# Second mixer of a two-layer streaming encoder: each projection weight split once for two or three blocks, queries kept in memory, all keys and values on chip, float32 values in column tiles

## The chip, the cores and the metric

The kernel runs on one core of a Trainium2 chip. The metric is the device time of one execution in microseconds (us). A core has a matmul engine (PE; its weight loads are shown as PEld), a vector engine (DVE), a scalar engine (ACT), a general engine (POOL), and a queue that issues the DMAs (SP). Each engine takes its own instructions in order and waits on semaphores for the others. Matmuls write to PSUM, from where DVE or ACT carry the results to the on-chip memory SBUF.

## The reference

Layer 0 is a gated linear recurrence with a feed-forward part, layer 1 a grouped-query attention over a sliding window with a feed-forward part. Each part normalises before and after. The change is in layer 1's attention and in the projections that feed it:

```python
k, v = jnp.split(rms_norm(x, kv_norm) @ w_kv, 2, axis=-1)
k = rope(k.reshape(B, T, B_KV_HEADS, B_HEAD_DIM), pos)
...
q = rope((h @ w_b_q[j]).reshape(B, T, B_Q_HEADS, B_HEAD_DIM), pos)
...
s = jnp.einsum('bnqkgd,bnskd->bnkgqs', q.astype(F32), k.astype(F32)) * (B_HEAD_DIM ** -0.5)
s = jnp.where(valid[None, :, None, None, None, :], s, -jnp.inf)
m = jnp.maximum(jnp.max(s, axis=-1, keepdims=True), sink)
p = jnp.exp(s - m)
denom = jnp.sum(p, axis=-1, keepdims=True) + jnp.exp(sink - m)
return jnp.einsum('bnkgqs,bnskd->bnqkgd', p / denom, v.astype(F32))
```

There are 1024 prompt frames and 32 sample frames, a model width of 1024, 16 query heads and 4 key/value heads of 64, a window of 128 frames in chunks of 64, everything in float32.

## The kernel before

The 1056 frames are cut into three blocks of 384, 384 and 288 columns (`BL`). A dense product in near-float32 accuracy is made of three matmuls in the type fp32r: both operands are split into a high part and a remainder, and high times high, high times remainder and remainder times high are summed (`mm_fm`, line 132; `mm_tm`, line 144). A weight comes in units of 128 x 1024 (512 KB): `wunit` loads one, ACT makes the high part `wh`, DVE the remainder `wl`; where a norm weight is multiplied in, this is done in four pieces of 256 columns (lines 97 and 98), else at once (lines 101 and 102). There are two buffers for loads (`wst`) and four each for `wh` and `wl`. Two units (`wpair`) make the weight of one projection of 256 output columns.

The second mixer begins at line 827 while the first feed-forward part (`f0`) still finishes block 2. For each block, `kproj` makes the keys of all four heads, `vproj1` the values of three row tiles, and `qproj` the queries of one key head (four query heads). Keys and queries go through `rope` (rotation: four products on DVE, two sums on POOL) and then through DRAM to reach the layout that the scores need. Each projection of a block splits its weight anew: 18 pairs in all. Keys have two buffers (`kb`), values six (`vt`), and a value is split into high part and remainder (`split_v`).

Attention takes 12 steps per block (four key heads g, three row tiles jl). `att_s` makes the scores of four query heads in plain float32, the two heads of an even and odd pair in two PSUM tiles (`sc`), first all of one tile, then all of the other; adds the mask by small bf16 matmuls (`mk`); takes maxima (`rm`), exponentials (`P`, ACT), sums and normalises `P` head by head. `att_t` transposes `P` and splits it (`pth`, `ptl`); `att_v` multiplies by the split values: one matmul gives 128 rows of which high and remainder parts stand in different halves, which ACT and DVE move and add (lines 1028 to 1031) before the result is split again (`xh`, `xl`). The step before is transposed and multiplied after the scores of the present one.

`plan` puts other work between: in block 0 the projections of block 1, in block 1 those of block 2 and the output projection `op1` of block 0, in block 2 the last query projection, the normalisation of block 0 and the output projection of block 1. The order in which each engine gets the instructions is made by a scheduler from this program order; pools decide what has to wait for a buffer.

Of the kernel before, what the change touches and what calls it, by code (L numbers as in the profile page):

```python
# [8 lines left out]
F32 = mybir.dt.float32  # L9
# [15 lines left out]
NB = 3  # L25
# [33 lines left out]
def build(nc, tc, I, O):  # L59
# [767 lines left out]
    apc, ap = pool("ap")  # L827
    kbs, kds, vts, cosin = [None] * NB, [None] * NB, [None] * 9, [None] * NB
# [4 lines left out]

    def split_v(vf, rows, vt):
        vv = vf[:rows].rearrange("p (g d) -> p g d", g=4)
        nc.scalar.copy(vt[:rows, :, 0:64], vv)
        nc.vector.tensor_tensor(vt[:rows, :, 64:128], vv, vt[:rows, :, 0:64].bitcast(F32), sub)
        return vt

    def rope(b, units, res):  # L840
# [25 lines left out]
    def kproj(b):  # L866
# [3 lines left out]
        yield from rope(b, wpair(I["wk"], 0, scale="kv"), r)  # L870
# [4 lines left out]
        kb = kbs[b] = ap.tile([128, 4, 512], F32, tag="kb", name="kb", bufs=2)  # L875
# [9 lines left out]
    def vproj1(b):  # L885
# [3 lines left out]
        units = wpair(I["wv"], 0, scale="kv")  # L889
        for jl in range(3):  # L890
# [4 lines left out]
            vf = tmp()[:, :256]  # L895
            nc.scalar.activation(vf[:rows], ps[:rows, :256], AF.Copy, scale=rts[b][:rows, jl:jl + 1])
            j = 3 * b + jl
# [4 lines left out]
            vts[j] = split_v(vf, rows, ap.tile([128, 4, 128], F32R, tag="vt", name="vt", bufs=6))  # L902
            if jl < 2:
                yield

    take(0)
    gk, gv = kproj(0), vproj1(0)
    go(gk)
    go(f0)
    go(gk, 2)  # L910
    go(gv)
    go(f0)
    go(gv)
    ap2c, ap2 = pool("ap2")
    mbc, mb = pool("mb1", "right")
    mbs[:] = [mb, mb, None]
    os = [None] * NB
    nx = [None] * NB
    with tc.tile_pool(name="aps", bufs=1, space=PSUM, reuse_waits="tile") as aps:
# [9 lines left out]
        vcf = tmp()[:, :256]  # L929
        nc.sync.dma_start(vcf, I["cv"])  # L930
        vc = split_v(vcf, 128, ap2.tile([128, 4, 128], F32R, name="vc"))
# [3 lines left out]
        qts = {}  # L935

        def qproj(b, g):
            W = BL[b][1]
            r = []
            yield from rope(b, wpair(I["wq"], g, scale="mix_pre1"), r)  # L940
            a = r[0]
            qd = tc.dram_tile([2, 2, 2, 32, W], F32, name=f"qd{b}_{g}")
            for hf in range(2):
                nc.sync.dma_start(qd[:, :, hf].rearrange("pi pr r t -> (pi pr) r t"), a[:, hf, :W])
            qt = ap2.tile([128, 2, W], F32, tag="qt", name="qt", bufs=4)
            nc.sync.dma_start(qt, qd.rearrange("pi pr hf r t -> (pr hf r) pi t"))
            qts[b, g] = qt

        def att_s(b, g, jl):
# [14 lines left out]
            pss = []  # L964
            for pr in range(2):
                ps = aps.tile([128, 512], F32, tag="sc", name="sc", bufs=2)
                pvw = ps.rearrange("p (h k) -> p h k", h=2)
                rsl = slice(pr * 64, pr * 64 + 64)
                for pi in range(2):
                    lhs = qts[b, g][rsl, pi, qs]  # L970
                    off = lo
                    for (kt_, k0, n) in keys:
                        nc.tensor.matmul(pvw[:rows, pi, off:off + n], lhs, kt_[rsl, g, k0:k0 + n],  # L973
                                         start=pi == 0 and off == lo, stop=samp, skip_group_check=True)
                        off += n
                if not samp:
                    if lo == 0:
                        nc.tensor.matmul(pvw[:, :, 0:64], mk[rsl, 0:128], mk[rsl, 128:256], start=False,
                                         stop=True, skip_group_check=True)
                    nc.tensor.matmul(pvw[:, :, 192:256], mk[rsl, 0:128], mk[rsl, 256:384], start=False,  # L980
                                     stop=True, skip_group_check=True)
                nc.vector.tensor_reduce(rm[:rows, pr:4:2], pvw[:rows, :, lo:kend], AX.X, ALU.max)
                pss.append(pvw)
# [13 lines left out]
            for hh in range(4):  # L997
                nc.vector.tensor_scalar(P[:rows, hh, lo:kend], P[:rows, hh, lo:kend], rs[:rows, hh:hh + 1], None, mult)  # L998
            return dict(b=b, g=g, rows=rows, qs=qs, vals=vals, lo=lo, P=P)

        def att_t(c):
            rows, P = c["rows"], c["P"]
# [3 lines left out]
            for (vt, n) in c["vals"]:  # L1006
# [5 lines left out]
                pth = ap2.tile([128, 512], F32R, tag="pth", name="pth", bufs=2)  # L1012
                ptl = ap2.tile([128, 512], F32R, tag="ptl", name="ptl", bufs=2)
                nc.scalar.copy(pth[:n, :N], ptp[:n, :N])
                nc.vector.tensor_tensor(ptl[:n, :N], ptp[:n, :N], pth[:n, :N].bitcast(F32), sub)  # L1015
                c["pt"].append((pth, ptl))

        def att_v(c):
            rows, g, qs, vals = c["rows"], c["g"], c["qs"], c["vals"]
            N = 4 * rows  # L1020
            oh, ol = os[c["b"]]
            pav = aps.tile([128, 512], F32, tag="pt", name="pav", bufs=2)
            for i, ((vt, n), (pth, ptl)) in enumerate(zip(vals, c["pt"])):
                nc.tensor.matmul(pav[:, :N], vt[:n, g, :], pth[:n, :N], start=i == 0, stop=False)  # L1024
                nc.tensor.matmul(pav[:, :N], vt[:n, g, :], ptl[:n, :N], start=False, stop=i == len(vals) - 1)  # L1025
            pw = pav[:, :N].rearrange("p (pi pr q) -> p pi pr q", pi=2, pr=2)
            ot = tmp()[:, :256].rearrange("p (a q) -> p a q", a=2)
            nc.scalar.copy(ot[0:64, :, :rows], pw[64:128, :, 0, :])
            nc.scalar.copy(ot[64:128, :, :rows], pw[0:64, :, 1, :])
            nc.vector.tensor_tensor(ot[0:64, :, :rows], ot[0:64, :, :rows], pw[0:64, :, 0, :], add)  # L1030
            nc.vector.tensor_tensor(ot[64:128, :, :rows], ot[64:128, :, :rows], pw[64:128, :, 1, :], add)
            nc.scalar.copy(oh[:, 2 * g:2 * g + 2, qs], ot[:, :, :rows])
            nc.vector.tensor_tensor(ol[:, 2 * g:2 * g + 2, qs], ot[:, :, :rows],
                                    oh[:, 2 * g:2 * g + 2, qs].bitcast(F32), sub)
# [3 lines left out]

        go(gv, 4)
        gq = [qproj(0, g) for g in range(4)]  # L1040
        for g in range(4):
            go(gq[g])
            if g in (1, 2):
                go(f0)
            go(gq[g])
        K, Vp, Q = {}, {}, {}
        for b in (1, 2):
            take(b)
            K[b], Vp[b] = kproj(b), vproj1(b)
            Q[b] = [qproj(b, g) for g in range(4)]  # L1050
# [14 lines left out]
        for b in range(NB):  # L1065
            os[b] = newx(b)
            prev = None
            for u in range(13):
                c = att_s(b, u // 3, u % 3) if u < 12 else None
                for f, n in plan[b][u]:  # L1070
                    go(f, n)
# [117 lines left out]
```

## Time and profile before

| what | us |
|---|---|
| median of 3 runs | 2756.64 |
| lowest and highest | 2746.61, 2760.08 |
| the profiled execution | 2753.39 |
| its span, first to last instruction | 2751.5 |

The profile is of one execution. A row of instructions names the line, the engine, the operation, what is written from what, the shapes and the count. A row of a timeline begins with its start in us from the span's start, then how long it took. In a row by group the busy time and the mean of one stand behind the bar, then the idle time before it and what ended that.

### The profile page before, as it was taken

How to read it: one execution, taken by the hardware profiler on the slowest of the kernel's cores; microseconds unless marked ns; L12 is line 12 of the kernel's file. 1: busy time of each engine (PE TensorE's matmuls, PEld its weight loads, DVE VectorE, ACT ScalarE, POOL GpSimd, SP SyncE). 2: the span in 40 equal slices, each digit the busy share in tenths (PEclk: the TensorE clock that was granted, in tenths of full speed). 3: DMA queues.
4: the chain of work that ended last, by engine and by line, in shares of the span. 5: the costliest groups of instructions: out<-in, count | busy, mean ns of one | idle time of the engine just before them, and what ended most of it. 6: DMA issues, size and time to landing. Idle time of an engine off the chain costs nothing. (4 is left out here: it accounts for less than half of the span.)

```text
span 2751.5 us, 44746 instructions
## 1 busy us (share of the span) xinstructions
PE 2613.9 (95%) x17528; PEld 2516.8 (91%) x17528; DVE 1613.5 (59%) x3770; ACT 1054.7 (38%) x2371; POOL 422.1 (15%) x648
## 2 busy tenths in 40 slices
PE   7999998998999999999997799989899999999997
PEld 6999997998999999999997777878899999999997
DVE  8777778778523333333478687987633333333466
ACT  5555555555332121212244365666332121212133
POOL 5442435232100000000133101111200000000012
PEclk9999998999999999999999899999899999999998
DMA  5332333334311111111245623323421111111254
GB/s 165 91 95 95 109 101 112 120 109 130 111 47 47 46 47 46 47 47 54 88 152 154 187 81 120 107 93 99 128 63 47 46 47 47 47 46 47 70 161 143
DMA packets 95644, 247.00 MB, mean 90 GB/s; under 512 B 10264, under 2 KB 46008, under 8 KB 95432
## 3 DMA queue, kind: packets, MB, share of 16 engines
q1 hardware_dynamic: 95432, 244.14, 28.8%
q8 instruction: 138, 2.26, 0.3%
q14 instruction: 74, 0.61, 0.1%
HBM read 220.01 MB, written 24.28 MB: 89 GB/s over the span
## 5 line engine op out<-in xcount | busy, mean ns | idle before, releaser
L132 PE MATMUL mm<-xh,wh 128*128 128x384 f32 (+1 forms) x3120 | 1031.1, 331 | 15.1 <-ACT xh L205 11.7
L132 PE MATMUL mm<-xh,wl 128*128 128x384 f32 (+1 forms) x3120 | 1021.3, 328 | 22.2 <-DVE wl L98 17.1
L132 PE MATMUL mm<-xl,wh 128*128 128x384 f32 (+1 forms) x3120 | 1021.8, 328 | 2.8 <-DVE xl L206 2.5
L132 PEld LDWEIGHTS mm<-xh,wl 128*128 128x128 f32 x3120 | 596.5, 191 | 29.6 <-DVE wl L98 22.7
L132 PEld LDWEIGHTS mm<-xh,wh 128*128 128x128 f32 x3120 | 596.8, 191 | 23.4 <-ACT xh L205 12.6
L132 PEld LDWEIGHTS mm<-xl,wh 128*128 128x128 f32 x3120 | 596.1, 191 | 10.3 <-DVE xl L206 7.3
L102 DVE TENSOR_TENSOR wl<-wst,wh 128x1024 fp32r<-128x1024 f32 (+1 forms) x301 | 371.4, 1236 | 255.0 <-ACT wh L101 253.3
L101 ACT CAST wh<-wst 128x1024 fp32r<-128x1024 f32 (+1 forms) x301 | 314.5, 1047 | 469.9 <-PE mm L132 413.6
L174 POOL TENSOR_TENSOR acc<-acc,tmp 128x384 f32<-128x384 f32 (+1 forms) x168 | 195.0, 1162 | 1834.4 <-ACT tmp L173 1824.4
L132 PE MATMUL mm<-gh,wl 128*128 128x384 f32 (+1 forms) x1056 | 342.4, 325 | 12.1 <-DVE wl L102 12.1
L132 PE MATMUL mm<-gh,wh 128*128 128x384 f32 (+1 forms) x1056 | 343.3, 326 | 3.9 <-ACT gh L283 2.8
L132 PE MATMUL mm<-gl,wh 128*128 128x384 f32 (+1 forms) x1056 | 343.1, 325 | 0.0
L328 DVE TENSOR_TENSOR mix<-mix,mm 128x384 f32<-128x384 f32 (+1 forms) x240 | 124.4, 520 | 237.1 <-PE mm L132 237.1
L281 DVE TENSOR_TENSOR tmp<-mm,rb 128x384 f32<-128x384 f32 (+1 forms) x132 | 68.8, 522 | 254.4 <-PE mm L132 254.3
L132 PEld LDWEIGHTS mm<-gh,wl 128*128 128x128 f32 x1056 | 200.0, 190 | 13.1 <-DVE wl L102 13.1
L132 PEld LDWEIGHTS mm<-gh,wh 128*128 128x128 f32 x1056 | 199.8, 189 | 5.7 <-ACT gh L283 3.8
L283 ACT CAST gh<-tmp 128x384 fp32r<-128x384 f32 (+1 forms) x132 | 64.2, 486 | 360.3 <-DVE tmp L282 360.3
L132 PEld LDWEIGHTS mm<-gl,wh 128*128 128x128 f32 x1056 | 200.1, 189 | 0.3 <-DVE gl L284 0.2
L144 PE MATMUL mm<-wh,xh 128*128 128x256 f32 (+1 forms) x648 | 187.0, 289 | 2.5 <-ACT vt L492 2.4
L280 ACT ACTIVATE tmp<-tmp 128x384 f32<-128x384 f32 (+1 forms) x132 | 65.8, 498 | 316.4 <-DVE tmp L279 316.4
L144 PE MATMUL mm<-wh,xl 128*128 128x256 f32 (+1 forms) x648 | 184.1, 284 | 0.0
L144 PE MATMUL mm<-wl,xh 128*128 128x256 f32 (+1 forms) x648 | 182.3, 282 | 0.5 <-DVE wl L98 0.5
(205 smaller groups left out, 3147.3 us busy)
## 6 DMA issues: line engine op xcount, KB each, us to landing
wst<-in_wfi SPq DMA_DIRECT2D x120, 512.0 KB
wst<-in_wfo SPq DMA_DIRECT2D x60, 512.0 KB
wst<-in_wfq SPq DMA_DIRECT2D x47, 512.0 KB
wst<-in_wi SPq DMA_DIRECT2D x24, 512.0 KB
wst<-in_wg SPq DMA_DIRECT2D x24, 512.0 KB
wst<-in_wao SPq DMA_DIRECT2D x24, 512.0 KB
wst<-in_wq SPq DMA_DIRECT2D x24, 512.0 KB
wst<-in_wbo SPq DMA_DIRECT2D x24, 512.0 KB
```

Source lines behind the costliest of these rows:

```text
L101: nc.scalar.copy(wh[:, s], st[:, s])
L102: nc.vector.tensor_tensor(wl[:, s], st[:, s], wh[:, s].bitcast(F32), sub)
L132: last_mm[0] = nc.tensor.matmul(ps[:, :W], w, x, start=i == 0, stop=i == n - 1)
L144: last_mm[0] = nc.tensor.matmul(ps[:rows, :256], x, w, start=i == 0, stop=i == n - 1)
L174: nc.gpsimd.tensor_tensor(acc[:, :W], acc[:, :W], q[:, :W], add)
L280: nc.scalar.activation(ta[:, :W], ta[:, :W], AF.Silu)
L281: nc.vector.tensor_tensor(tb[:, :W], pb[:, :W], rb[:, :W], mult)
L283: nc.scalar.copy(gh[:, c0:c0 + W], tb[:, :W])
L328: nc.vector.tensor_tensor(dst, dst, ps[:, :W], add)
```

## The change

It does six things.

1. A weight pair is made outside the projections and handed to them: one key weight and one value weight serve blocks 0 and 1, another pair block 2; each of the four query weights serves all three blocks. That is 8 pairs for 18.
2. Both key and value projections of blocks 0 and 1, then those of block 2, and eight of twelve query projections are made ahead of the attention. The four left (blocks 1 and 2, heads 2 and 3) are spread over block 0's steps; block 1's steps carry the output projection of block 0, block 2's its normalisation and the output projection of block 1.
3. Rotated queries stay in DRAM tiles (`qds`) until `qload` brings them, four buffers.
4. All three key blocks have their own buffer, all nine value tiles too; values are kept in float32 without a split.
5. Scores alternate between the two PSUM tiles, so between the lower and upper 64 rows of the array. The product with the values is in float32, with 64 columns of weights: even heads write the lower, odd heads the upper 64 rows of PSUM. `P` transposed is copied (`pts`), by ACT for the first value tile and by DVE for the second, and the result is split straight from PSUM.
6. `P` is normalised by one product over four heads.

```diff
-    def kproj(b):
+    def kproj(b, units):
...
-        yield from rope(b, wpair(I["wk"], 0, scale="kv"), r)
+        yield from rope(b, units, r)
...
-        kb = kbs[b] = ap.tile([128, 4, 512], F32, tag="kb", name="kb", bufs=2)
+        kb = kbs[b] = late_pool[b].tile([128, 4, 128 + W], F32, name=f"kb{b}")
...
-            vts[j] = split_v(vf, rows, ap.tile([128, 4, 128], F32R, tag="vt", name="vt", bufs=6))
+            vf = vts[j] = ap.tile([128, 256], F32, tag="vt", name="vt", bufs=9)
...
-            cosin[b] = [ap.tile([128, 384], F32, tag=t, name=t, bufs=1) for t in ("cosr", "sinr")]
+            cosin[b] = [rp[0].tile([128, W], F32, name=f"{t}{b}") for t in ("cosr", "sinr")]
...
-        a = ap.tile([128, 2, 384], F32, tag="ra", name="ra", bufs=1)
+        a = rp[0].tile([128, 2, 384], F32, tag="ra", name="ra", bufs=2)
...
+            for pi in range(2):
+                off = lo
+                for (kt_, k0, n) in keys:
+                    for pr in range(2):
+                        rsl = slice(pr * 64, pr * 64 + 64)
+                        nc.tensor.matmul(pss[pr][:rows, pi, off:off + n], qts[b, g][rsl, pi, qs],
+                                         kt_[rsl, g, k0:k0 + n], start=pi == 0 and off == lo, stop=samp,
+                                         skip_group_check=True)
...
-            for hh in range(4):
-                nc.vector.tensor_scalar(P[:rows, hh, lo:kend], P[:rows, hh, lo:kend], rs[:rows, hh:hh + 1], None, mult)
+            nc.vector.tensor_tensor(P[:rows, :, lo:kend], P[:rows, :, lo:kend],
+                                    rs[:rows].unsqueeze(2).broadcast_to([rows, 4, kend - lo]), mult)
...
-                nc.scalar.copy(pth[:n, :N], ptp[:n, :N])
-                nc.vector.tensor_tensor(ptl[:n, :N], ptp[:n, :N], pth[:n, :N].bitcast(F32), sub)
+                if i == 0:
+                    nc.scalar.copy(pts[:n, :N], ptp[:n, :N])
+                else:
+                    nc.vector.tensor_copy(pts[:n, :N], ptp[:n, :N])
...
-                nc.tensor.matmul(pav[:, :N], vt[:n, g, :], pth[:n, :N], start=i == 0, stop=False)
-                nc.tensor.matmul(pav[:, :N], vt[:n, g, :], ptl[:n, :N], start=False, stop=i == len(vals) - 1)
+                for pr in range(2):
+                    nc.tensor.matmul(pav[pr * 64:pr * 64 + 64], vt[:n, g * 64:g * 64 + 64], ph[:, :, pr, :],
+                                     start=i == 0, stop=i == len(vals) - 1, skip_group_check=True)
...
+        for i, q in enumerate(late):
+            plan[0][3 * i] = plan[0][3 * i + 1] = [(q, 1)]
+        p, o = OP[0], OP[1]
+        for u in (1, 2, 3, 4, 6, 7, 8, 10, 11, 12):
+            plan[1][u] = [(p, 1)]
+        plan[2] = {u: [(p, 1)] for u in range(6)}
+        for u in range(4, 12):
+            plan[2].setdefault(u, []).append((o, 1))
```

Three places show how the order moves. First DVE, in the query projections ahead of the attention; before, `wl` (L98) is the remainder of a query weight, and L858 to L861 are the rope:

```order
L98 SCALAR_TENSOR_TENSOR wl<-wst,pv,wh 128x256 x3
L858 TENSOR_TENSOR ra<-mm,cosr 128x384
L859 TENSOR_TENSOR tmp<-mm,sinr 128x384
L98 SCALAR_TENSOR_TENSOR wl<-wst,pv,wh 128x256 x5
L860 TENSOR_TENSOR tmp<-mm,sinr 128x384
L861 TENSOR_TENSOR ra<-mm,cosr 128x384
L98 SCALAR_TENSOR_TENSOR wl<-wst,pv,wh 128x256 x7
```

The same place with the change, from the end of the splits of the second query weight (rope is L855 to L858 there):

```order
L98 SCALAR_TENSOR_TENSOR wl<-wst,pv,wh 128x256 x12
L855 TENSOR_TENSOR ra<-mm,cosr_16603 128x384
L856 TENSOR_TENSOR tmp<-mm,sinr_16604 128x384
L857 TENSOR_TENSOR tmp<-mm,sinr_16604 128x384
L858 TENSOR_TENSOR ra<-mm,cosr_16603 128x384
L855 TENSOR_TENSOR ra<-mm,cosr_16692 128x384
L856 TENSOR_TENSOR tmp<-mm,sinr_16693 128x384
L857 TENSOR_TENSOR tmp<-mm,sinr_16693 128x384
L858 TENSOR_TENSOR ra<-mm,cosr_16692 128x384
```

Before, every rope stands between the eight pieces of the next weight; now two blocks are roped behind each other and the pieces stand in a bundle ahead of them.

Second PE, inside an attention step: transposes (`ptp`), scores (`sc`), masks (`mk`) and values (`pav`), before, in block 0:

```order
L1009 MATMUL ptp<-ident,P 128x128 x8
L973 MATMUL sc<-kb,qt 128x256 x2
L978 LDWEIGHTS mk
L978 MATMUL sc<-mk 128x2x64
L980 LDWEIGHTS mk
L980 MATMUL sc<-mk 128x2x64
L973 MATMUL sc<-kb,qt 128x256
L1024 MATMUL pav<-pth,vt 128x512
L1025 MATMUL pav<-ptl,vt 128x512
```

And with the change, in block 1:

```order
L1023 MATMUL ptp<-ident,P 128x128 x8
L983 MATMUL sc<-kb_16240,qt 128x256 x2
L1041 MATMUL pav<-pts,vt 64x256 x4
L983 MATMUL sc<-kb_16240,qt 128x256 x2
L993 LDWEIGHTS mk
L993 MATMUL sc<-mk 128x2x64
```

Four value matmuls of 512 columns over the whole array have become four of 256 columns over half of it each, the scores of both tiles stand together, and the masks follow behind them.

Third SP, which issues the DMAs, at the end of the projections ahead of the attention, before (`qd` is the DRAM copy of a query, `qt` the tile that the scores read):

```order
L944 DMA qd_1_16573<-ra 4x32x384 x2
L90 DMA wst<-in_wq 128x1024
L946 DMA qt<-qd_1_16573 128x2x384
L90 DMA wst<-in_wk 128x1024 x2
L944 DMA qd_2_16667<-ra 4x32x384 x2
L90 DMA wst<-in_wv 128x1024
L946 DMA qt<-qd_2_16667 128x2x384
```

With the change, after the second key weight:

```order
L90 DMA wst<-in_wq 128x1024 x2
L911 DMA qd_1_17067<-ra 4x32x384 x2
L957 DMA qt<-qd_1_17067 128x2x384
L911 DMA qd_1_17131<-ra 4x32x384 x2
L90 DMA wst<-in_wbo 128x1024
```

Before, each query is followed by the loads of a further weight; now two blocks' queries are written per weight, and the first weight of the output projection already stands there.

More of the change, by code (lines that the diff above doesn't have):

```diff
@@ L1026, in att_v @@
[L1026 to L1032, printed above, removed]
@@ L1047, in build, with wq @@
[L1047 to L1050, printed above, removed]
+        def wq(g):
+            return wpair(I["wq"], g, scale="mix_pre1")
+        uq = wq(0)
+        run(qproj(0, 0, uq))
+        qload()
+        go(f0)
+        run(qproj(1, 0, uq))
+        go(f0)
+        take(2)
+        uk = wpair(I["wk"], 0, scale="kv")
+        run(kproj(2, uk))
+        run(qproj(2, 0, uq))
+        uv = wpair(I["wv"], 0, scale="kv")
@@ L1069, in build @@
                 c = att_s(b, u // 3, u % 3) if u < 12 else None
-                for f, n in plan[b][u]:
+                if u % 3 == 0 and u > 0 and order:
+                    qload()
+                for f, n in plan[b].get(u, ()):
                     go(f, n)
```

141 lines of the change are left out of this document (69 added, 72 removed).

## The prediction

> **What bounds the kernel now.** I read the page first, then busy time by stretch, then the waits of the second mixer, then its instructions.
>
> ```profile
> span 2751.5 us, 44746 instructions
> PE 2613.9 (95%) x17528; PEld 2516.8 (91%) x17528; DVE 1613.5 (59%) x3770; ACT 1054.7 (38%) x2371; POOL 422.1 (15%) x648
> ```
>
> A PE that is 95% busy seems to leave nothing to win, but records of pipelined matmuls overlap: they last longer than they lie apart. What counts is the distance between starts. The next rows give, for each stretch, length, busy time of PE, PEld, DVE, ACT and POOL, granted clock, DMA share and GB/s:
>
> ```profile
> 1483.00:1560.00 77.00, 66.25 (x359) 60.36 (x357) 57.87 (x138) 33.67 (x84) 20.55 (x22) 0.91 0.57 170
> 1560.00:1912.00 352.00, 318.54 (x1900) 271.82 (x1899) 285.59 (x748) 222.28 (x674) 47.95 (x48) 0.94 0.34 104
> 1483.00:1912.00 429.00, 384.79 (x2257) 332.18 (x2255) 343.46 (x886) 255.96 (x757) 68.49 (x70) 0.94 0.38 116
> 1912.00:2000.00 88.00, 79.15 (x440) 75.34 (x440) 59.65 (x126) 36.53 (x70) 23.23 (x22) 0.86 0.40 122
> ```
>
> The change touches 1483 to 1912: a front of projections for block 0 (to 1560), then 36 attention steps with the other projections and out-projections as filler. DVE is busy 286 of the 352 us of the steps. In both parts PE waits for DVE and ACT:
>
> ```profile
> PE pav L1024 <- DVE ptl L1015: 16.0, 18, 5.0
> PEld mm L132 <- DVE wl L98: 15.5, 14, 5.6
> PE mm L132 <- DVE wl L98: 10.7, 10, 5.3
> PE sc L973 <- ACT P L992: 9.2, 3, 7.9
> ```
>
> These are totals, times and the longest wait: the split of a weight (wl), the split of the probabilities (ptl) and the exponentials (P). The granted clock of 0.91 to 0.94 comes on top, since PE's gaps lower it. So the mixer is bound by PE and DVE together, each held up by the other.
>
> PE's own need is read from starts, count and distance:
>
> ```profile
> 1498.87 0.28 PE L144 MATMUL mm<-wh,xh 128*128 128x256 f32 x1
> ...
> 1501.46 0.28 PE L144 MATMUL mm<-wh,xl 128*128 128x256 f32 x1
> ...
> 1587.11 1.13 PE L973 MATMUL sc<-kb,qt 64*128 64x256 f32 x4
> 1588.07 0.22 PE L978 MATMUL sc<-mk 64*128 64x128 bf16 x1
> 1588.13 0.22 PE L980 MATMUL sc<-mk 64*128 64x128 bf16 x1
> 1588.27 0.38 PE L144 MATMUL mm<-wh,xh 128*128 128x256 f32 x1
> ...
> 1738.29 0.30 PE L132 MATMUL mm<-xl,wh 128*128 128x288 f32 x1
> ...
> 1741.20 0.29 PE L132 MATMUL mm<-xh,wl 128*128 128x288 f32 x1
> 1741.33 1.04 PE L1009 MATMUL ptp<-ident,P 128*128 128x128 f32 x8
> 1742.30 1.24 PE L973 MATMUL sc<-kb,qt 64*128 64x256 f32 x6
> ...
> 1809.08 0.34 PE L132 MATMUL mm<-xh,wh 128*128 128x384 f32 x1
> ...
> 1812.44 0.34 PE L132 MATMUL mm<-xl,wh 128*128 128x384 f32 x1
> ```
>
> From first to last there are 22, 22 and 19 steps: 0.118 us for a 256-column matmul, 0.132 for 288, 0.177 for 384. Four float32 score passes take 0.96 us (1587.11 to 1588.07), 0.24 each; each float32 score matmul is two passes. Eight transposes take 0.97. A mask follows a mask after 0.06, but a full-array matmul follows a mask after 0.14: a change of tiling costs about 0.09.
>
> **The change, part by part.** Dense matmuls neither vanish nor appear; they move.
>
> *Front.* It now holds three key, nine value and eight query pieces: 384 matmuls of 384 columns (68.0 us), 144 of 288 (19.0) and 216 of 256 (25.5), 112.5 us. The order shows a weight split before the projection that needs it, and one split serving two or three projections. One switch is late: the second value weight takes the slots that the last query projection has just freed, about 0.5 + 0.5 us for the first piece on ACT and DVE and 8 pieces at 0.5 against 0.35 of PE work, 2.5 us. The DVE burst of the feed-forward's last normalisation (at most 16.5 us by the rows of L234, L235 and L206 below, which are for the wider block) now lies beside 144 value matmuls, 17 us, whose eviction is ACT's; if that cover failed, the longest wait on wl above, 5.3 us, would return. With 3 us, an estimate, for normalisation matmuls and small waits the front is **118 us**.
>
> *Queues.* SP takes its transfers in order. The front asks for 16 weight loads of 0.5 MB and, by the shapes, some 7 MB of keys, queries and spilled blocks: 15 MB in 118 us, 130 GB/s, below the 170 that the old front reached, so I cost it at nothing; were it not hidden, rival 3 is what it would look like. The query loads of later blocks stand before out-projection weights on SP and wait for one of four query buffers, free once the third step of a head group has its scores; two weight buffers are filled ahead of them. The rotation tables are loaded and scaled five times instead of three, on POOL, which is busy 21 of 77 us in the front.
>
> *Splits, ropes and evictions.* DVE and ACT have in the steps (line, shapes, count, busy us, mean ns):
>
> ```profile
> L98 DVE SCALAR_TENSOR_TENSOR wl<-wst,pv,wh 128x256 fp32r<-128x256 f32 x92 | 42.0, 495 | 2.0 <-ACT wh L97 1.8
> L97 ACT ACTIVATE wh<-wst,pv 128x256 fp32r<-128x256 f32 x91 | 39.7, 508 | 20.4 <-DMA wst<-in_wv 13.0 <-PE mm L132 4.3 <-PE mm L144 1.9
> L1015 DVE TENSOR_TENSOR ptl<-ptp,pth 128x512 fp32r<-128x512 f32 x60 | 39.5, 678 | 0.7 <-ACT pth L1014 0.3
> L982 DVE TENSOR_REDUCE rm<-sc 128x2 f32<-128x512 f32 x56 | 37.5, 683 | 5.9 <-PE sc L980 5.5
> ...
> L102 DVE TENSOR_TENSOR wl<-wst,wh 128x1024 fp32r<-128x1024 f32 x20 | 24.1, 1215 | 2.0 <-ACT wh L101 2.0
> ...
> L1031 DVE TENSOR_TENSOR tmp<-tmp,pav 64x256 f32<-64x256 f32 x32 | 13.6, 425 | 0.5
> L1030 DVE TENSOR_TENSOR tmp<-tmp,pav 64x256 f32<-64x256 f32 x32 | 13.1, 410 | 9.5 <-ACT tmp L1029 9.3
> ...
> L206 DVE SCALAR_TENSOR_TENSOR xl<-mixb,pv,xh 128x384 fp32r<-128x384 f32 x8 | 6.5, 817 | 0.0
> ...
> L235 DVE TENSOR_TENSOR mixb<-mixb,xo 128x384 f32<-128x384 f32 x8 | 5.0, 638 | 1.2 <-DMA xo<-xsb 1.2
> ...
> L234 DVE SCALAR_TENSOR_TENSOR mixb<-mixb,pv,rb 128x384 f32<-128x384 f32 x8 | 4.6, 606 | 0.0
> ```
>
> Out of the steps go all scaled splits (42.0 us of DVE, 39.7 of ACT), half of L1015 (about 20: one plain copy remains, on DVE for the second value tile only), L1030 and L1031 (26.7) and seven of eleven ropes (four operations of about 0.5, 14). DVE falls from 286 to about 183 us. ACT loses its splits and the two moves between halves, and falls further below PE.
>
> *One P operation for four.* The four old ones and the nearest row for the new shape, L102's 1.215 us for 1024 columns:
>
> ```profile
> 1744.85 1.13 DVE L998 TENSOR_SCALAR P<-P,rs 128x256 f32<-128x256 f32 x4
> ```
>
> The sum takes no change (bounds: 0.3 us less a step, four fixed costs saved, to 0.1 more). The Trainium skill speaks against this edit: VectorE: DVE Perf Modes, section "Mode 2×_2P — use both read ports for one tensor", says that a float32 operation with a scalar can run at two elements per cycle from SBUF and one with two tensors only at one, which by its 0.96 GHz is an estimate of 0.53 us before and 1.07 after, 17 us more DVE over the steps; by it the forecast would be some 2 us later, since DVE bounds only block 2's first steps. The trace disagrees for the old form: 0.28 us for 256 columns is one element per cycle.
>
> *Tiles on PE.* Scores now alternate between the two row halves, value matmuls between two column halves. No value matmul of this shape is in the trace; the nearest is the first mixer's float32 one with 64 columns of weights, alternating halves:
>
> ```profile
> 312.45 0.77 PE L672 MATMUL psB<-ZZ,K 128*64 128x96 f32 x12
> 313.00 0.42 PE L675 MATMUL psB<-Q,K 128*64 128x64 f32 x2
> ```
>
> Twelve passes of 96 columns start in 0.55 us, 0.046 each, where 0.24 x 96/256 = 0.090 would be serial: the halves run in pairs. I take pairs: eight passes fill five slots (one half starts a slot later), 1.2 us for values (four passes of 0.23 before, no gain) and 1.3 with masks for scores (2.1 before). Serial would be 1.9 and 2.1. A full step needs 1.3 + 0.97 + 1.2 = 3.5 us of PE; 28 full and 8 short steps (1.7) 112 us. The program order counts 185 changes of tiling against 123: 62 x 0.09 = 6 us more. Filler is 96 matmuls of 384, 96 of 288 and 384 of 384 (two out-projections): 98 us. Sum 216 us, so PE is the longest by 33.
>
> *What is left uncovered.* Steps without filler (seven in blocks 0 and 1) run at the loop score, maximum, exponentials, next score: 1.3 + 2 x 0.68 + four exponentials of about 0.46 + small work and hand-overs 0.8 = 5.3 against 3.5, 12 us. In block 2's first four steps block 0's normalisation (8 x (0.82 + 0.64 + 0.61) = 16.5 us of DVE) has no matmuls beside it: 16. Start and end: 6. Attention is **250 us**.
>
> *Sum.* The last feed-forward matmul starts at 1486.4, so before has 425.5 us to 1912; after 118 + 250 = 368. Out-projection tail (88 us) and all else keep their order: cost 0. The gain is 57: 2751.5 - 57 = 2694.5, with 2 us around the span (profiled execution 2753.4) **2696 us**. The median shown, 2756.6, lies 3 us higher. The transfers now taken once (20 loads of 512 KB fewer) gain nothing more by themselves.
>
> **The rivals.**
> 1. *PE near its floor*: uncovered parts shrink to 10, front 115: 341, 2669 us. For: DVE has 33 us to spare. Against: block 2 starts without matmuls.
> 2. *Tiles serial*: 1.5 us more a full step, 42: 2738. Against: L672.
> 3. *Front as ragged as before*: 1486.5 to 1560, 73.5 us, for one key, three value and four query pieces, 240 x 0.177 + 72 x 0.118 = 51 us, 1.44 times; 112.5 x 1.44 = 162, 44 more: 2740. For: it keeps the order split, project, rope on one DVE. Against: 8 splits for 20 pieces. Half of it: 2718.
> 4. *Slower: latency, not work, sets the step.* Before, 352 / 36 = 9.8 us a step with filler inside. If the chain of scores, maximum, exponentials, transposes and values keeps that, the projections moved forward are simply added: 118 + 352 = 470, 2798. It decides from (425.5 - 118) / 36 = 8.5 us a step. For: both score banks are now needed at once. Against: the chain above is 5.3, and the waits on ptl and wl lose their cause.
> That the change doesn't do what it says is excluded by the order: 64 scaled pieces per engine for 144, and paired tiles.
>
> **How the numbers follow.** Forecast 0.64 (2675 to 2722); rival 1 0.12; rival 2 0.07; rival 3 0.12, half of it at the half price; rival 4 0.05. Range 2658 to 2732: rival 1 and half of rival 3 inside, serial tiles and rival 4 outside. 0.5% is about what a measurement of this kernel tells from no change: 14 us. Faster 0.64 + 0.12 + 0.07 + half of rival 3 = 0.89; same 0.06; slower 0.05.
>
> **What would show it.** Right: a front of about 118 us with PE starts 0.177 apart and hardly a wait on wl; steps of 6.9 us on average; DVE about 183 us in the steps; eight value passes in about 1.2 us. Wrong: waits on wl between projections (rival 3), passes 0.24 apart (rival 2), scores waiting for P in steps with filler (rival 4).

## The result, and the profile after

The changed kernel takes 2711.0 us (median of 4 runs, 2708.0 to 2716.4) against 2755.4 us for the kernel before, now of 4 runs too. The ratio is 0.985, with a 95% interval of 0.983 to 0.987. The two medians lie 44 us apart, but by the ratio and by the traces below it is faster by about 40 us, where 57 were forecast. The page of the changed kernel begins so:

```profile
span 2714.5 us, 44432 instructions
PE 2602.9 (96%) x17664; PEld 2494.4 (92%) x17664; DVE 1534.2 (57%) x3464; ACT 977.3 (36%) x2177; POOL 428.1 (16%) x652
```

DVE lost 79 us and ACT 77, twice what the kernel gained: most of that work had been hidden. The next rows are busy time by stretch (length, busy us of PE, PEld, DVE, ACT and POOL, granted clock, DMA share, GB/s). The first is the front, from the start of the last feed-forward matmul to the first score, the second the 36 attention steps, the third the out-projection tail:

```profile
1493.65:1613.50 119.85, 116.46 (x767) 113.35 (x765) 72.94 (x162) 36.83 (x92) 37.42 (x40) 1.00 0.58 171
...
1613.50:1878.00 264.50, 247.00 (x1597) 186.79 (x1597) 186.54 (x407) 140.39 (x467) 37.07 (x32) 0.95 0.24 73
1878.00:1966.00 88.00, 79.42 (x447) 75.77 (x445) 60.14 (x126) 36.91 (x71) 23.26 (x22) 0.86 0.38 118
```

The front has grown as forecast and runs at the full clock; the steps have shrunk from 350 to 264 us. PE's waits in the front, and then PE's and its weight loads' in the steps (total, times, longest):

```profile
PE mm L189 <- DVE dm L185: 1.5, 2, 1.0
PE mm L132 <- DVE tmp L856: 1.2, 1, 1.2
PE mm L132 <- DVE wl L98: 0.7, 2, 0.3
```

```profile
PE ptp L1023 <- DVE P L1010: 5.4, 7, 2.2
PE pav L1041 <- DVE pts L1030: 4.3, 3, 2.2
PE pav L1041 <- ACT pts L1028: 2.4, 6, 0.8
```

```profile
PEld pav L1041 <- ACT pts L1028: 11.2, 28, 1.2
PEld sc L983 <- issue: 9.4, 32, 0.8
```

Almost nothing is left of the waits on the weight splits (10.7 us) and on the split probabilities (16.0). What is left are waits for the normalised P and for the copies of the transposes.

To compare traces I cut each at three instructions: the start of the last feed-forward matmul, of the first score and of the last value matmul.

| kernel | last FFN matmul | front | steps | front + steps | to the last matmul | median, us |
|---|---|---|---|---|---|---|
| before | 1486.4 | 73.6 | 350.4 | 424.0 | 830.3 | 2755.4 |
| after | 1493.6 | 119.8 | 264.1 | 383.9 | 826.1 | 2711.0 |
| E1 attention edits only | 1488.5 | 69.3 | 343.5 | 412.8 | 825.6 | 2741.9 |
| E2 unpaired order | 1486.5 | 119.6 | 277.6 | 397.2 | 825.8 | 2723.0 |
| E3 four P operations | 1487.0 | 120.1 | 262.5 | 382.6 | 827.1 | 2707.6 |
| E4 grouped order | 1483.2 | 119.7 | 286.0 | 405.7 | 827.8 | 2729.7 |
| E5 out-projection early | 1490.5 | 120.3 | 257.2 | 377.5 | 824.9 | 2702.0 |
| E6 one score tile | 1484.2 | 120.0 | 256.8 | 376.8 | 826.3 | 2701.9 |
| E7 = E5 and E6 | 1484.6 | 119.8 | 249.1 | 368.9 | 831.0 | 2695.7 |
| E8 matmuls of zeros added in the second feed-forward | 1481.9 | 119.9 | 266.5 | 386.4 | 872.4 | 2753.2 |
| E9 split for each projection | 1484.9 | 143.7 | 275.9 | 419.6 | 825.1 | 2745.1 |
| E10 = E7, copies on ACT | 1485.9 | 120.0 | 249.7 | 369.7 | 829.8 | 2697.3 |
| E11 ten loads more | 1490.0 | 130.8 | 268.8 | 399.6 | 825.0 | 2724.4 |
| E12 ten splits more | 1495.8 | 126.8 | 264.2 | 391.0 | 825.5 | 2720.2 |

Up to the first column every kernel issues the same instructions in the same order; its 14 us of scatter (1481.9 to 1495.8) are between executions. So the 7.2 us by which the profiled execution of after starts its front late are no effect of the change, nor are the 4.2 it gains at the end (824.9 to 831.0 over all but E8, whose added work lies there). The change itself is the fifth column: 424.0 - 383.9 = 40.1 us. Differences between kernels are read there below, and whole times beside them. E8 gives a measure for their scatter: up to the second feed-forward PE has the same instructions there as in the changed kernel, and they take 386.4 us against 383.9. Two or three us between two rows of this column therefore say nothing.

### The profile page after: what moved, and what is told of

Its sections match the earlier page's. It is cut to its first block, busy times and chain, and to the rows that moved or that the text cites. A ratio compares the mean times of both kernels' runs of the same rounds, so it can differ in the third digit from the quotient of the medians.

```text
span 2714.5 us, 44432 instructions
## 1 busy us (share of the span) xinstructions
PE 2602.9 (96%) x17664; PEld 2494.4 (92%) x17664; DVE 1534.2 (57%) x3464; ACT 977.3 (36%) x2177; POOL 428.1 (16%) x652
## 4 chain that ended last, share of the span: by engine, by line
PE 74%; DVE 15%; ACT 5%; DMA 4%; issue 2%; POOL 1%; SPq 0%; POOLq 0%; ACTq 0%; DVEq 0%
PE mm L132 63%; PE mm L144 5%; DVE wl L102 2%; ACT wh L101 1%; DVE xl L206 1%; PE sc L983 1%; PE pav L1041 1%; DVE wl L98 1%; DVE mixb L235 1%; DVE mix L234 1%; DVE mixb L234 1%; DVE mix L235 1%; PE ptp L1023 1%; PE po L729 1%; ACT P L1005 1%
## 5 line engine op out<-in xcount | busy, mean ns | idle before, releaser
L132 PE MATMUL mm<-gl,wh 128*128 128x384 f32 (+1 forms) x1056 | 343.5, 325 | 0.0
```

The costliest lines, as they stand in the source:

```text
L132: last_mm[0] = nc.tensor.matmul(ps[:, :W], w, x, start=i == 0, stop=i == n - 1)
```

## The experiments

The theory from the two traces: both halves of the change earn; the missing 14 us of the steps (264 where 250 were forecast) are changes of tiling on PE that cost more than the forecast's 0.09 us. The rival: PE's work is as forecast, and the latency of the chain from scores to values sets the pace.

**E1, one half alone.** The kernel before, with the attention edits only:

```diff
-            vf = tmp()[:, :256]
+            vf = vts[j] = ap.tile([128, 256], F32, tag="vt", name="vt", bufs=6)
...
-            vts[j] = split_v(vf, rows, ap.tile([128, 4, 128], F32R, tag="vt", name="vt", bufs=6))
```

`att_s`, `att_t` and `att_v` are those of the changed kernel.

> The kernel before with the attention half of the change alone: float32 values in column tiles, scores alternating between row halves, one P operation, no split of the probabilities; projections stay per block inside the steps. Theory A (both halves earn: the attention edits take about 46 us off DVE and pair the tiles, the projection edits take the scaled splits out of the steps): about 2735 us, half of the gain of 44. Rival B (only the projections matter): within 5 us of the kernel before, 2750 to 2760. Rival C (only the attention edits matter): 2705 to 2715, as the changed kernel.

Measured: 2741.9 us, ratio 0.996 (0.9945 to 0.998); front and steps lose 11.2 of the 40.1 us. Between A and B: the attention edits are worth something over a quarter, although they take 48 us off DVE in the steps, which now read as follows, with PE's waits behind:

```profile
1557.80:1901.30 343.50, 315.22 (x2024) 253.20 (x2024) 237.73 (x525) 181.55 (x564) 51.35 (x48) 0.93 0.34 106
```

```profile
PE sc L964 <- ACT P L986: 13.7, 4, 6.9
PE pav L1022 <- ACT pts L1009: 5.1, 8, 1.6
PE pav L1022 <- DVE pts L1011: 4.9, 4, 2.2
```

The waits of values have fallen from 16.0 to 10.0 and those of scores risen from 9.2 to 13.7. The seven longest waits of PE in the steps add up to 32 us before and to 27 here, so little of the 48 us that DVE no longer does was what PE waited for.

**E2, pairs undone.** In the changed kernel, scores and values again half after half:

```diff
-            for pi in range(2):
+            for pr in range(2):
+              for pi in range(2):
...
-                    for pr in range(2):
```

> The changed kernel with scores issued one row half after the other and values one column half after the other, as the scores were before. If the pairs run at the same time and PE sets the pace of the steps, 8 passes of 0.215 us take the place of 4 slots in scores and in values: 1.7 us a full step, 28 x 1.7 + 8 x 0.85 = 55 us at most, 30 to 55 us slower. If the chain scores, maximum, exponentials, transposes, values sets the pace (rival), the extra passes lie in PE's waits: under 15 us slower. If tiles did not pair at all: no change.

Measured: 2723.0 us, 13.3 us more in front and steps. That would speak for latency, but the trace shows that the edit was only half an undoing, since the instructions of the two halves were still ordered together where both were ready. Counting score and value passes that start within 25 ns of the one ahead: 88 and 136 pairs (of 160 and 136) in the changed kernel, 29 and 66 here. So 129 passes more have a slot of their own, at 0.209 us 27 us of PE, and 13 of them show. That is neither theory's extreme: about half of PE's additional work shows as time.

The count also shows that in the changed kernel itself 72 of the 160 score pairs do not form (E6, whose expectation takes 93 as formed where this count has 88).

**E3, the P operation undone.**

```diff
-            nc.vector.tensor_tensor(P[:rows, :, lo:kend], P[:rows, :, lo:kend],
-                                    rs[:rows].unsqueeze(2).broadcast_to([rows, 4, kend - lo]), mult)
+            for hh in range(4):
+                nc.vector.tensor_scalar(P[:rows, hh, lo:kend], P[:rows, hh, lo:kend], rs[:rows, hh:hh + 1], None, mult)
```

> The changed kernel with P normalised by four operations with a per-partition scalar, as before. By the row of before (four took 1.13 us) against the one operation of after (1.19 us mean): DVE busy in the steps within 3 us, time within 5 us of the changed kernel. If a float32 operation with a scalar ran at two elements per cycle: 17 us less DVE in the steps, 0.6 us an operation shorter, and about 2 us less time.

Measured: 2707.6 us; its interval (0.982 to 0.985) overlaps that of the changed kernel. The groups of P's normalisation, first of the changed kernel, then of this one (count, busy us, mean ns):

```profile
L1010 DVE TENSOR_TENSOR P<-P,rs 128x1024 f32<-128x1024 f32 x28 | 36.1, 1289 | 0.4
```

```profile
L1011 DVE TENSOR_SCALAR P<-P,rs 128x256 f32<-128x256 f32 x112 | 39.8, 418 | 0.5
```

28 steps take 1.29 us each in one operation and 39.8 / 28 = 1.42 in four, on average; where nothing disturbs them it is 1.22 (the median) and 1.14. The edit is worth nothing either way. The Trainium skill (VectorE: DVE Perf Modes, section "Mode 2×_2P — use both read ports for one tensor") would have the four at two elements per cycle, by an estimate 0.53 us a step; the measured 1.42, and 1.14 undisturbed, contradict it for this form.

**E4, fewer changes of tiling.** PE's order in the steps is fixed to whole groups, each queued behind the last matmul of the one ahead:

```diff
+                with after_dense():
                     c = att_s(b, u // 3, u % 3) if u < 12 else None
...
+                with after_dense():
                     for f, n in plan[b].get(u, ()):
                         go(f, n)
...
+                    with after_dense():
                         att_t(prev)
+                    with after_dense():
                         att_v(prev)
```

> The changed kernel with PE's order in the steps fixed to whole groups: scores and masks, projection or out-projection work, transposes, values. Changes of tiling fall from 184 to 110; no work is added or left out. Theory A (each change of tiling costs PE about 0.26 us, worked out as 266 us of the steps less 196 of matmuls at their distances less 21 of long waits, over 185 changes): 74 x 0.26 = 19 us less, of which the lost freedom to fill waits takes some back: 5 to 19 us faster than the changed kernel. Rival B (a change costs the 0.09 us of the prediction, and the chain's latency sets the pace): 7 us less PE work, more waits of values for the copies of the transposes: 0 to 25 us slower.

Measured: 2729.7 us, 22 us more in front and steps. PE's waits in the steps are now these:

```profile
PE pav L1041 <- ACT pts L1028: 15.0, 27, 1.4
PE ptp L1023 <- DVE P L1010: 10.9, 6, 3.5
PE sc L983 <- ACT P L1005: 9.7, 7, 4.5
PE pav L1041 <- DVE pts L1030: 8.4, 11, 2.0
```

The sum over PE's distances above 0.45 us between two starts, each less 0.26, rises from 21 us to 53; without it the steps fall from 243 to 233. Put down to the 74 changes less alone, these 10 us would be 0.13 each, half the 0.26 of theory A. But 128 score pairs form here where 88 did, which at 0.209 us a pass is 8 of the 10 us, so E4 leaves no clear price for a change; E8 gives one. Theory A falls as to size. What the grouping costs, 32 us more in long waits, is three times what it saves: PE needs the freedom to put projection work into a step's waits.

**E8, the price of a change measured by itself.** In the second feed-forward, where PE is the bound, matmuls of zeros are added into the running sums, in three shapes, one kind to a group of 24 (`m` counts groups):

```diff
+                    if probe[0] is not None and n == 24 and i in (8, 16):
+                        z, m = probe[0], probe[1] % 4
+                        if m == 1:
+                            nc.tensor.matmul(ps[:, 0:64], z[:, 0:128], z[:, 0:64], start=False, stop=False)
+                        elif m == 2:
+                            nc.tensor.matmul(ps[:, 0:64], z[0:64, 0:128], z[0:64, 0:64], start=False, stop=False)
+                        elif m == 3:
+                            nc.tensor.matmul(ps[0:64, 0:64], z[:, 0:64], z[:, 0:64], start=False, stop=False)
```

> The changed kernel with 66 additional bf16 matmuls of 64 columns of zeros of each of three shapes inside the first projections of the second feed-forward, where PE is the bound and the starts lie 0.177 us apart: on the whole array, on 64 rows, on 64 columns. The result doesn't change. A whole-array one should cost its own time, about 0.06 us. For one on half the rows or columns, two changes of tiling come on top: 0.24 us in all if a change costs 0.09 us (the prediction), 0.32 to 0.44 us if it costs 0.13 to 0.19 (the first matmul behind a change also starts its successor late, as the rows of the changed kernel look). The time rises by 36 us or by 46 to 62.

Measured: one run of 2753.2 us, 42 more. PE's timeline (start, duration) around one on half the rows, then around one on the whole array:

```profile
2014.67 0.33 PE L132 MATMUL mm<-xl,wh 128*128 128x384 f32 x1
2014.94 0.20 PE L139 MATMUL mm<-zt 64*128 64x64 bf16 x1
2015.07 0.44 PE L132 MATMUL mm<-xh,wl 128*128 128x384 f32 x1
2015.35 0.33 PE L132 MATMUL mm<-xh,wh 128*128 128x384 f32 x1
...
2046.40 0.33 PE L132 MATMUL mm<-xh,wh 128*128 128x384 f32 x1
2046.57 0.20 PE L137 MATMUL mm<-zt 128*128 128x64 bf16 x1
2046.61 0.42 PE L132 MATMUL mm<-xl,wh 128*128 128x384 f32 x1
2046.88 0.34 PE L132 MATMUL mm<-xh,wl 128*128 128x384 f32 x1
```

From the first row to the fourth it is 0.68 us with a change there and back, 0.48 without, 0.35 undisturbed. These are also the medians of the 44 of each kind that stand among matmuls of 384 columns; for half of the columns it is 0.70. A change costs (0.68 - 0.48) / 2 = 0.10 us, and 0.11 for columns: the forecast's 0.09 was right. The total of 0.24 that the expectation draws from it was not, at 0.33 and 0.35, because the small matmul alone costs 0.13 and not 0.06. This 0.13 has nothing to do with tiling: 0.04 is the matmul itself, and 0.09 comes because the matmul behind it holds PE for 0.27 until the next start instead of 0.175. The next weight load, 0.19 us long, would not fit beside a matmul of 0.04; that reading was not tested.

**E5, work beside block 0's normalisation.** Cut into pieces of 8 us, the start of block 2 stands out (columns as above):

```profile
1778.00:1786.00 8.00, 5.20 (x30) 3.12 (x29) 7.62 (x17) 5.19 (x16) 0.99 (x1) 1.00 0.30 97
1786.00:1794.00 8.00, 4.64 (x32) 2.59 (x30) 7.18 (x15) 4.70 (x15) 2.47 (x3) 0.59 0.29 100
1794.00:1802.00 8.00, 6.63 (x36) 4.07 (x36) 7.64 (x16) 4.51 (x16) 2.56 (x2) 0.77 0.31 101
1802.00:1810.00 8.00, 4.62 (x22) 3.15 (x22) 7.21 (x17) 3.95 (x14) 3.00 (x2) 0.65 0.32 98
1810.00:1818.00 8.00, 7.79 (x36) 7.59 (x36) 4.59 (x20) 2.53 (x11) 0.27 (x2) 0.71 0.00 0
```

In the first four rows DVE is busy over 7 of 8 us and PE 4.6 to 6.6; from 1786 the granted clock lies below 0.8, and it stays there until 1818, after DVE's pressure has ended. E5 puts block 1's out-projection there; its result takes the place of the key tiles of blocks 0 and 1, as the one buffer of that size is still in use:

```diff
-        for u in range(4, 12):
+        for u in range(0, 8):
             plan[2].setdefault(u, []).append((o, 1))
+        mixes[1] = lambda: Halves(*[ap.tile([128, 4, 512], F32, tag=f"kb{i}", name=f"mix1{i}") for i in range(2)])
```

> The changed kernel with block 1's out-projection matmuls in the steps u = 0 to 7 of block 2 instead of u = 4 to 11 (its result goes into the space of the key tiles of blocks 0 and 1, so that it need not wait for block 0's buffer). Same work. Theory A (in the first 45 us of block 2 DVE is the bound, since block 0's last normalisation, 16.5 us of DVE, has no matmuls beside it; PE waits there and its granted clock falls to 0.5 to 0.8): these steps cost no more with the matmuls inside, the later ones lose them, 5 to 12 us faster than the changed kernel, and the clock of block 2 near 1.00. Rival B (DVE's turn-around inside each step sets the pace, and matmuls in it only delay transposes and values): within 3 us, or slower by up to 10.

Measured: 2702.0 us, ratio 0.982 (0.980 to 0.983); the steps lose 6.9 us. The same stretch now reads:

```profile
1778.00:1786.00 8.00, 8.00 (x51) 6.45 (x51) 7.75 (x16) 5.32 (x17) 1.52 (x2) 1.00 0.32 101
1786.00:1794.00 8.00, 6.26 (x46) 4.83 (x44) 8.00 (x17) 7.11 (x19) 3.17 (x3) 1.00 0.42 141
1794.00:1802.00 8.00, 7.10 (x48) 6.28 (x48) 8.00 (x16) 5.99 (x18) 3.71 (x4) 1.00 0.36 127
1802.00:1810.00 8.00, 8.00 (x63) 6.39 (x59) 7.20 (x14) 5.27 (x17) 3.64 (x4) 1.00 0.60 173
```

206 PE instructions in 32 us where there were 120, at the full clock, with DVE as busy as before. PE's waits from the start of block 2 to 1818 fall from 11 us to 2.6. Theory A held. How much of the 7 us is filled waiting and how much the clock was not separated.

**E6, score pairs.** The second score bank is read by the last exponentials, so the first row half's scores start while the other half's must wait. One tile for both banks lets none start before both are free:

```diff
-            pss = [aps.tile([128, 512], F32, tag="sc", name="sc", bufs=2).rearrange("p (h k) -> p h k", h=2)
-                   for _ in range(2)]
+            sc = aps.tile([128, 2, 2, 256], F32, tag="sc", name="sc", bufs=1)
+            pss = [sc[:, 0], sc[:, 1]]
```

> The changed kernel with both score banks as one tile, so that no score starts before both banks are free. 93 of the 160 pairs of score passes ran together in the trace of the changed kernel; the others ran alone, the first row half's while the second bank was still being read by the exponentials. Theory A (PE sets the pace in blocks 0 and 1): up to 67 passes of 0.209 us less, 14 us of PE, of which 3 to 12 us show as time saved; at least 130 pairs. Rival B (the early half was a head start for the maximum, so the chain grows by 0.65 us a step where it is the bound): 5 to 20 us slower.

Measured: 2701.9 us, ratio 0.983 (0.981 to 0.984); the steps lose 7.3 us, and 152 of 160 pairs form. Eight passes of one step in the changed kernel, and in this one with what follows them:

```profile
1681.75 2.01 PE L983 MATMUL sc<-kb,qt 64*128 64x256 f32 x8
1683.69 0.65 PE L1041 MATMUL pav<-pts,vt 128*64 128x256 f32 x4
```

```profile
1671.76 1.13 PE L983 MATMUL sc<-kb,qt 64*128 64x256 f32 x8
1672.72 0.28 PE L993 MATMUL sc<-mk 64*128 64x128 bf16 x4
```

1.94 us against 0.96 from the first pass to what follows. Waiting for both banks is cheaper than a head start. Nearly all of it comes in blocks 0 and 1 (from the first score to the first maximum of block 2, `ng`, 159.8 us, where the changed kernel takes 167.1).

**E7, both.**

> Both edits: block 1's out-projection early in block 2, and the two score banks as one tile. If both theories A hold: 8 to 24 us faster than the changed kernel; if each edit is worth nothing: within 4 us of it.

Measured: 2695.7 us, ratio 0.980 (0.979 to 0.981), steps 249.1: the two add up, 15 us below the changed kernel, and this is the fastest version. By whole times each edit alone hardly stands clear of the changed kernel's interval (0.983 to 0.987); the two together do. **E10** added to it both copies of the transposes on ACT in block 2:

```diff
-                if i == 0:
+                if i == 0 or c["b"] == 2:
                     nc.scalar.copy(pts[:n, :N], ptp[:n, :N])
```

> Block 1's out-projection early in block 2 and the two score banks as one tile (the kernel that took 2695.7 us), and in block 2 both copies of the transposes on ACT, none on DVE. If DVE still bounds the first steps of block 2 with block 0's normalisation: 0.68 us less DVE in eight steps, 2 to 5 us faster than 2695.7. If not: within 2 us, or slower by 1 to 4, since ACT then makes both copies one after the other ahead of the values (0.6 us a step).

Measured: 2697.3 us, 0.980 (0.979 to 0.982): nothing. It fits that with matmuls beside it DVE's work there no longer sets the end; but if ACT's second copy cost what DVE saves, it would look the same, and that was not tested.

**E9, the split for each projection.** The changed kernel's order, but every projection loads and splits for itself:

```diff
-    uk = wpair(I["wk"], 0, scale="kv")
+    uk = lambda: wpair(I["wk"], 0, scale="kv")
...
     def rope(b, units, res):
+        units = units()
```

> The changed kernel with every projection loading and splitting its weight for itself, as before, and all else as changed: the order of the projections, the front, the steps. 20 loads of 512 KB and 80 scaled pieces on ACT and on DVE (about 0.5 us each) come back, most of them in the front. Theory A (the split once is what lets the front run at PE's pace): the front's DVE work rises from 73 to about 105 us of 120 and waits on the split return, front 130 to 160 us, 15 to 45 us slower than the changed kernel. Rival B (moving the projections out of the steps is what counts, and splits hide beside the longer run of projections): under 6 us slower.

Measured: 2745.1 us, 35.7 us more in front and steps: theory A by its time. Beside E1 (2741.9) this is the main result on the projections: moving them alone gains nothing; serving several from one weight gains some 34 us. Sharing a weight without moving the projections was not run. But ACT's waits around the front do not name the split:

```profile
ACT wh L97 <- DMA wst<-in_wq: 40.6, 12, 6.5
...
ACT wh L97 <- DMA wst<-in_wv: 17.5, 4, 8.7
...
ACT wh L97 <- DMA wst<-in_wk: 13.4, 4, 6.7
```

ACT waits 72 us for transfers, 65 of them in the front itself, where it is 22 in the changed kernel. DVE then waits for ACT, and PE 12 us for ACT's half of the weight and 6 for DVE's. Two more kernels take loads and splits apart.

**E11 and E12, loads or splits.** Ten of the front's shared weights are loaded again but not split (E11), or split again from the staging buffer but not loaded (E12):

```diff
+    st = wp.tile([128, 1024], F32, tag="wst", name="wst", bufs=2)
+    nc.sync.dma_start(st, arr[2 * i + k])
+    nc.gpsimd.tensor_copy(junk, st[:, 0:1])
```

```diff
+    nc.scalar.activation(wh[:, s], st[:, s], AF.Copy, scale=p)
+    nc.vector.scalar_tensor_tensor(wl[:, s], st[:, s], p, wh[:, s].bitcast(F32), mult, sub)
```

> The changed kernel with ten weight loads of 512 KB more in the front (the key and value weights for block 1, two query weights for blocks 1 and 2), into the same two staging buffers, read only by a one-column copy on GpSimd; splits stay single. It takes the loads of the kernel that split each weight anew apart from its splits. Theory A (the loads are what that kernel waited for: its ACT waited 72 us for transfers in the front's window): 5 MB more in 120 us ask for 213 GB/s where 192 was the most that kernel reached, front 130 to 145 us, 10 to 25 us slower than the changed kernel. Theory B (the splits on ACT and DVE are what it waited for): under 4 us slower.

> The changed kernel with the same ten weights of the front split a second (third) time from the staging buffer, without loading them again: 40 scaled pieces more on ACT and on DVE, about 20 us of each. Theory B (splits): front 130 to 140 us, 10 to 20 us slower than the changed kernel. Theory A (loads): under 4 us slower, except for what comes from the staging buffers, which are held until the last split, so that the next weight's load starts later.

Measured: 2724.4 us (0.987 to 0.992) with loads, 2720.2 (0.984 to 0.989) with splits; in front and steps 15.7 and 7.1 us more, 11.0 and 6.9 of it in the front, where the additional work lies. The fronts:

```profile
1490.00:1620.80 130.80, 120.70 (x765) 116.71 (x763) 71.21 (x160) 37.50 (x92) 38.40 (x50) 0.96 0.63 192
```

```profile
1495.80:1622.60 126.80, 119.85 (x765) 116.04 (x763) 91.08 (x202) 53.61 (x132) 37.91 (x40) 0.97 0.54 161
```

Both cost. With loads the front comes into theory A's range, with DVE no busier than in the changed kernel; with splits it stays below theory B's. So the loads cost more, 11 us against 7 in the fronts, but not by much: by whole times it is 13 against 9, and the intervals overlap. The splits' share is not certain: the whole time's interval overlaps that of the changed kernel (0.983 to 0.987), and holding the staging buffers delays the next load there too. Nor is it shown that the loads cost by their rate: E11's front moved 192 GB/s on average, but up to 343 in slices of 3 us. SP waited 11.8 us ahead of the additional loads until a split had freed a staging buffer, and POOL sat 34 us in E11's own copies until their transfers came, with the sums of the ropes behind them.

## Why the prediction was right or wrong

Right as to direction and range; the gain was 40 us of a forecast 57. Of the 17 us between, 1.8 lie in the front and 14.1 in the steps; the rest is the end of the stretch, which the forecast set to 1912 in the kernel before and the table to its last value matmul at 1910.4. Point by point:

- **Front, 118 us**: 119.8. PE waits 0.7 us on a weight split, and the feed-forward's last normalisation was covered. The transfers were estimated at 15 MB, 130 GB/s; 20.5 MB moved at 171 GB/s, and PE's three waits in the front name none of them.
- **DVE in the steps, 183 us**: 186.5. That less DVE work there makes the steps short was only partly the reason: of the 10.7 us of waits on weight splits in the kernel before, 9.4 lie in the front, and E1, with 238 us of DVE, saves 11 us.
- **One P operation for four, no change**: no change (E3). Its time, 1.29 us on average, lies 0.06 above the upper bound (1.13 + 0.1); the median, 1.22, within it.
- **Value pairs, 1.2 us**: all 136 form, four passes in 0.58 us (a start at 1675.05, the next instruction at 1675.63), eight in 1.16.
- **Changes of tiling, 0.09 us each**: 0.10 to 0.11 (E8). My theory of 0.26, formed on the trace of after, was wrong; the prediction's row was right.
- **Score pairs, 1.3 us a step with masks**: this step failed. It took every pair as formed because the order alternates, and did not ask when the second bank comes free, though rival 4 names that both banks are needed at once. 72 of 160 pairs did not form. Priced by E6: 7.3 us.
- **Uncovered parts, 34 us**: the places were partly wrong, and one size. The forecast's own terms give blocks 0 and 1 (20 x 3.5 + 4 x 1.7 + 63.7 of filler + 4 + 12 + 3) 159.5 us and block 2 (8 x 3.5 + 4 x 1.7 + 34 + 2 + 16 + 3) 89.8. The trace has 167.1 (to block 2's first maximum) and 97.0. In blocks 0 and 1 E6 returns the difference (159.8). In block 2 the 16 us left PE idle for a third of the first 32 us, and such waiting was forecast, but the fall of the clock that came with it was not: up to 1818 PE works at 0.59 to 0.77. Its price is somewhere within the 7 us; E5, which takes waiting and clock away together, brings block 2 to 88.6 and saves 6.9 over all steps. With both edits (E7) the steps take 249.1 us.
- **"The transfers now taken once gain nothing more by themselves"**: wrong as a cause. The front's 118 us are only to be had without the 20 loads: ten of them, 0.5 MB each, cost 11 us in the front (E11), by rate, by buffers or by E11's own copies. The sum did not suffer, as the front was worked out from PE starts in the new order.
- **Rivals**: PE near its floor is excluded by the steps, 264 us where it needed 226 (341 - 115); tiles serial is excluded by the starts; a ragged front is what E9 gives, at about half its price (24 us more instead of 44); latency decides only where PE's order leaves nothing to fill in (E4), and the steps take 7.3 us, below the 8.5 from which it would have decided.

## What to carry to other kernels

An alternating order makes pairs on PE only if both outputs come free together; count the pairs in the trace before counting on them. When several uses share one weight, price the loads that fall away as well as the splits: here the loads were taken as free and cost at least as much. Put PE work beside a burst of VectorE work, not behind it: here a PE that was busy 5 of 8 us fell to a clock of 0.59, and paid again after the burst.

## What the runs showed of the hardware

The clock falls without a long pause. Here are three rows of PE from the start of block 2 in the changed kernel (timeline; in brackets the idle time ahead and its end):

```profile
1785.77 1.06 PE L1023 MATMUL ptp<-ident,P 128*128 128x128 f32 x8 [1.47 <-DVE P L1010]
...
1789.29 1.12 PE L1041 MATMUL pav<-pts,vt 128*64 128x256 f32 x4 [1.24 <-DVE pts L1030]
...
1794.37 1.95 PE L1023 MATMUL ptp<-ident,P 128*128 128x128 f32 x8 [2.19 <-DVE P L1010]
```

Eight transposes took 1.06 us at 1785.8 and 1.95 at 1794.4, and four value passes went from 0.65 to 1.12. The longest pause in the ten microseconds ahead of the slow passes at 1789.3 was 1.47 us, and PE was busy for 5.2 of the 8 us to 1786. The Trainium skill (TensorE: Matmul & The Clock Gate, section "Why this matters for your kernels") asks for no idle gap of PE over about 3 us; in this trace the clock fell to 0.59 (1786 to 1794) behind gaps at most half as long, one behind another. Whether the gaps alone do it, or also that much of the work between them uses half of the array (64*128 and 128*64 in the rows), no run here separates.
